# Retention's output stores issued from GpSimd instead of SyncE, and a rearranged turning of the first rows, in a streamed encoder block

## The chip, the cores and the metric

The kernel runs on one core of a Trainium2 chip. The metric is the device time of one execution in microseconds (us), taken as the median of several runs. TensorE is called PE here, VectorE DVE, ScalarE ACT, GpSimd POOL and SyncE SP, as the profile does.

## The reference

One layer of a hybrid encoder block over 2048 tokens of width 1024, all in float32. A norm, one wide projection, two branches (chunked attention and retention), two gated output projections, a merge, one more projection, the residual, and a norm at the end:

```python
h = rms_norm(x, norm_gain[l])
proj = jnp.einsum('bsd,df->bsf', h, w_in[l])
q_a, k_a, v_a, g_a, q_r, k_r, v_r, g_r, m_a, m_r = split_columns(proj)
o_a = chunk_band_attention(q_a, k_a, v_a, rel_bias[l])
branch_a = jnp.einsum('bsf,fd->bsd', o_a * jax.nn.silu(g_a), w_out_attn[l])
...
o_r = retention_chunkwise(qr, kr, v_r, gn_gain[l]) 
branch_r = jnp.einsum('bsf,fd->bsd', o_r * jax.nn.silu(g_r), w_out_ret[l])
mixed = jax.nn.sigmoid(m_a) * branch_a + jax.nn.sigmoid(m_r) * branch_r
x = x + jnp.einsum('bsd,de->bse', mixed, w_out[l])
return rms_norm(x, final_gain)
```

Retention is computed in chunks of 64 tokens with a state that is carried from chunk to chunk, and its output `o` is normalised by head: `(o - mean) * rsqrt(var + eps)`. The kernel sums the squares of `o` for that (`o2` below).

## The kernel before

All intermediate results that do not fit on the chip go through scratch tensors in device memory, and every stage streams its inputs back. Matrix products are done in pairs of a high and a low part of each float32 operand (`wh`, `wl`; `sh`, `sl`; `o2h`, `o2l`): ACT casts the high part, DVE or POOL subtracts it from the original for the low part, and PE multiplies high by high, low by high and high by low. The big projections (`ps_p_*`, `ps_g_*`, `ps_out_*`) use a seven-product scheme for two by two blocks.

**The order of work** is the order in which the program emits it: each engine runs its instructions strictly in that order. `fill(n)` emits n groups of projection matmuls, and between them stand the steps of attention or of retention, so that PE always has projection work while the other engines prepare the next step. `later(n, fn)` emits `fn` n groups later, and `put(n, dst, src)` (line 258) is `later` of a DMA on SP's queue.

**Buffers.** In each stage a ring of tiles of 128x512, made by `E(name)` (line 114), holds all short-lived values; in retention it has 12 of them (`E_RET`, line 57). A tile that is handed out again makes the first writer wait until everything that read or wrote the old content is through, a DMA that still reads it included. Which slot a new tile gets is decided when the program is built, and not by the source line alone.

**Start-up** (`start_up`, line 711). The first four row tiles `xa[0..3]` of x are loaded, each 128 tokens in two halves of 512 columns. `squares` takes the sum of squares (ACT one half, DVE or ACT the other), `chain` the reciprocal root (`n_a`), `scale` multiplies the rows by it, and `turn` transposes 128x128 blocks on PE into four tiles `pa0_0..3`. The norm weights `gains` (8x128) are transposed on PE too, and ACT writes them, times a constant, to `ng` (line 812). `hi` and `lo` then apply `ng` and split the turned rows into `R`, the operand of all projections; `prime(1)` (line 814) casts the first weights. PE has nothing to do until the rows come, so `spin(n)` gives it n transposes of the identity, whose result nobody reads. Before the change, the spare turns and the turned gains lie in one tile, called `gains`.

**Retention** (`retention`, line 632) runs twice, over the first and the second half of the tokens (at 560 to 720 us and 1306 to 1480 us), with 16 steps each: a step is one pair of heads and 256 tokens. In a step PE makes the scores `sr` of a coming step, DVE masks them (`sm`), ACT casts `sh`, POOL makes `sl`, and PE multiplies `sh` and `sl` with the values `vr` into `o`. `evacuate` (line 1777) then has ACT copy `o` to `oz` and its square to `o2` (shown as tile `o` too), stores `oz` to the scratch `ors` (256 KB, lines 1787 to 1791), and has ACT cast `o2h` and POOL make `o2l`, which PE sums into `ssq` in the next step. POOL also makes `t_g` and `wl_g` for the projection that fills the step. In the second half POOL issues eight DMAs of its own, `state<-sts` and `sstk<-sks`; all other loads and stores of retention are issued by SP.

Of the kernel before, what the change touches and what calls it, by code (L numbers as in the profile page):

```python
# [16 lines left out]
ALU = mybir.AluOpType  # L17
# [4 lines left out]
P = 128  # L22
SEQ = 2048
DM = 1024
# [49 lines left out]
def hybrid_kernel(  # L74
# [30 lines left out]
    def r32(ap):  # L105
        return ap.bitcast(F32)

    def ACC(name):
        return ps_acc.tile([P, 512], F32, tag="acc", name=name)
# [4 lines left out]
    def E(name, dt=F32, shape=(P, 512)):  # L114
        return epool[0].tile(list(shape), dt, tag="e", name=name)

    def TR(name):
        return xpool[0].tile([P, 512], F32, tag="tr", name=name)
# [34 lines left out]
    pe, act, dve, pool = Ordered(nc.tensor), Sometimes(nc.scalar), Sometimes(nc.vector), Sometimes(nc.gpsimd)  # L153
# [3 lines left out]
    ident = const.tile([P, P], F32, name="ident")  # L157
    make_identity(nc, ident)
    gn = const.tile([P, HEADS], F32, name="gn")
    ng = const.tile([P, 8], F32, name="ng")  # L160
# [84 lines left out]
    def later(n, fn):  # L245

        order[0] += 1
        deferred.append((steps[0] + n, order[0], fn, free[0]))
        deferred.sort(key=lambda e: e[:2])
# [8 lines left out]
    def put(lag, dst, src):  # L258

        later(lag, lambda: dma(dst, src))  # L260
# [355 lines left out]
    def prime(n):  # L616

        while ready[0] < min(n, len(seq)):
            _, ch, k = seq[ready[0]]
            ch.prepare(k)  # L620
            ready[0] += 1
            if ahead[0] and strict[0] and ready[0] + 1 < len(seq):
                _, ch, k = seq[ready[0] + 1]
                if isinstance(ch, Strassen):
                    ch.sums(k)
# [85 lines left out]
    def start_up():  # L711

        ch = jobs[0].chunks[:2]
        xa, xb = ([[E(f"x{i}_{t}_{f}") for f in range(2)] for t in range(4)] for i in "ab")
# [20 lines left out]
        nn = {i: [small.tile([P, 4], F32, tag=f"n{v}", bufs=2, name=f"n{v}_{i}") for v in range(4)] for i in "ab"}  # L735

        def squares(xs, i, t, on_dve=False, fs=range(2)):
            for f in fs:
                junk = junks[on_dve].bitcast(BF16)[:, 512 * f:512 * f + 512]
                if on_dve:  # L740
                    dve.tensor_tensor_reduce(
                        junk, xs[t][f], xs[t][f], 1.0, 0.0, ALU.mult, ALU.add, ss[i][:, t, f:f + 1]
                    )
                else:
                    act.activation(junk, xs[t][f], AF.Square, accum_out=ss[i][:, t, f:f + 1])

        def chain(i, t0, t1):
            deviation(ss[i][:, t0:t1], *(n[:, t0:t1] for n in nn[i]))

        def scale(xs, i, t, f, on_act=False):  # L750
            r = nn[i][0][:, t:t + 1]
            if on_act:
                act.mul(xs[t][f], xs[t][f], r)
            else:
                dve.tensor_scalar(xs[t][f], xs[t][f], r, None, ALU.mult)

        def turn(ps, k, xs, f, ts=range(4)):

            for t in ts:
                pe.transpose(ps[:, t * P:(t + 1) * P], xs[t][f][:, k * P:(k + 1) * P], ident)  # L760
# [13 lines left out]
        gains = E("gains")[0:8, 0:P]  # L774
# [11 lines left out]
            quarter(c, "b22")  # L786
            rows(xb, B, 2 + c)

        spare = ACC("gains")
        turned = spare[:, 0:8]  # L790

        def spin(n):
            for _ in range(n):
                pe.transpose(spare[:, P:2 * P], ident, ident)

        spin(38)
        ps = [TR(f"pa0_{k}") for k in range(4)]
        for t in (0, 1):
            squares(xa, "a", t, False, (0,))
            squares(xa, "a", t, True, (1,))  # L800
        chain("a", 0, 2)
        for t in (0, 1):
            scale(xa, "a", t, 0)
        for k in range(4):
            turn(ps[k], k, xa, 0, (0, 1))
        pe.transpose(turned, gains, ident[0:8, 0:8])
        spin(10)
        squares(xa, "a", 2)
        squares(xa, "a", 3, False, (0,))
        squares(xa, "a", 3, True, (1,))  # L810
        chain("a", 2, 4)
        act.mul(ng, turned, DM ** 0.5)
        scale(xa, "a", 2, 0)
        prime(1)
        scale(xa, "a", 3, 0, True)
        for k in range(4):
            turn(ps[k], k, xa, 0, (2, 3))
# [814 lines left out]
    def retention(s, ps_ret):  # L1632
# [8 lines left out]
        for n in range(3):  # L1641
            t = epool[0].tile([P, 2, 2, T], F32R, tag=f"q{n}", bufs=1, name=f"qr_{s}_{n}")
# [112 lines left out]
        def sure(here):  # L1755

            while not here():
                emit()
# [18 lines left out]
        def evacuate(p, st, ops):  # L1777
            b, un = st // 2, st % 2
            nm = f"{p}_{st}"
            got = []  # L1780

            def out_():
                oz = E(f"oz_{nm}")
                o2 = E(f"o2_{nm}")
                act.copy(oz, ops)
                act.activation(o2, ops, AF.Square)
                put(
                    2,
                    orscr[p][b][:, :, un * T:(un + 1) * T].rearrange("i p t -> p i t"),
                    oz.rearrange("p (i t) -> p i t", i=2),  # L1790
                )
                later(2, lambda: high(o2))

            def high(o2):
                got.append(E(f"o2h_{nm}", F32R))
                act.copy(got[0], o2)
                later(2, lambda: low(o2))

            def low(o2):
                got.append(E(f"o2l_{nm}", F32R))  # L1800
                pool.tensor_tensor(got[1], o2, r32(got[0]), ALU.subtract)

            later(1, out_)

            def sums():
                sure(lambda: len(got) == 2)
                r = 4 * p + st - 4 * s
                for n, t in enumerate(got):
                    pe.matmul(
                        ssq, ohr[:, ONE - r:ONE - r + 16], t, start=not begun[0],  # L1810
                        stop=(p == 3 and st == 4 * s + 3 and n == 1), skip_group_check=True,
                    )
                    begun[0] = True

            return sums
# [105 lines left out]
    for j in (jobs[0], jobs[2]):  # L1921
        for i in range(2):
            hook(j.name, i, 1 if j is jobs[2] else (0, 1, 1), lambda j=j, i=i: j.chunks[2].load([i]))
    start_up()
    ahead[0] = AHEAD

# [133 lines left out]
```

## Time and profile before

| what | value |
|---|---|
| median of 3 runs | 1889.68 us (1889.32 to 1890.17) |
| profiled execution | 1889.91 us, of which its span in the profile is 1888.1 us |
| PE busy | 1863.9 us (99% of the span) |
| DVE, ACT, POOL busy | 1367.6, 933.6 and 672.8 us |
| DMA queue of POOL (q0) | 448 packets, 1.05 MB |
| DMA queue of SP (q1) | 253552 packets, 363.28 MB |

All instructions come from helpers, so every row has the same line, L143, and is told apart by the names of its tiles (numbers are left out: `sl` stands for every tile whose name begins so). In a row of the timeline stand the start, the duration, the engine, the operation with output and inputs, and in brackets the idle time before it and what ended it. "DMA to landing" runs from the issue of a DMA to its last byte.

### The profile page before, as it was taken

The numbers are of one execution on the slowest core, as the hardware profiler recorded it, in microseconds if no ns is written. First come the engines' busy times: TensorE is split into PE (matmuls) and PEld (weight loads), VectorE is DVE, ScalarE is ACT, GpSimd is POOL, SyncE is SP. The second block draws the span as 40 slices with busy tenths as digits, with TensorE's granted clock in tenths as the row PEclk, the third lists the DMA queues.
The fourth block names the chain that finished last, engine by engine and source line by source line (L and its number), as shares of the span: only waits on it lengthen the run. The fifth ranks groups of instructions, "written<-read, shape, count | busy, mean of one in ns | idle before, by whom it ended". The sixth has DMA issues, their size and how long they took to land. (4 is left out here: it accounts for less than half of the span.)

```text
span 1888.1 us, 30822 instructions
## 1 busy us (share of the span) xinstructions
PE 1863.9 (99%) x10197; PEld 1603.3 (85%) x10197; DVE 1367.6 (72%) x2464; ACT 933.6 (49%) x1931; POOL 672.8 (36%) x604
## 2 busy tenths in 40 slices
PE   9999999999999999999999999999999999999998
PEld 7899889888888888799889888888888888888886
DVE  6879888677656658889798677765656766767665
ACT  7555554666654555443333666664455321223544
POOL 0102106455646562001105545555564100002775
PEclk9999999999999999999999999999999999999999
DMA  6586886666559987776776656555999999986674
GB/s 201 163 287 188 278 274 216 186 190 190 178 150 271 272 236 261 235 224 200 223 251 198 193 151 187 178 152 143 273 267 292 312 357 345 324 299 219 210 224 142
DMA packets 319295, 431.58 MB, mean 229 GB/s; under 512 B 28360, under 2 KB 193056, under 8 KB 319136
## 3 DMA queue, kind: packets, MB, share of 16 engines
q1 hardware_dynamic: 253552, 363.28, 60.0%
q10 hardware_dynamic: 65136, 65.28, 11.5%
q8 instruction: 81, 1.33, 0.3%
q0 software_dynamic: 448, 1.05, 0.2%
q14 instruction: 78, 0.64, 0.1%
HBM read 283.93 MB, written 145.57 MB: 227 GB/s over the span
## 5 line engine op out<-in xcount | busy, mean ns | idle before, releaser
L143 POOL TENSOR_SCALAR pr<-pr,rsum 128x640 f32<-128x640 f32 (+4 forms) x128 | 99.5, 777 | 195.5 <-DVE rsum L143 141.9
L143 DVE TENSOR_TENSOR ptl<-tp,pth 128x512 fp32r<-128x512 f32 (+1 forms) x168 | 100.2, 597 | 92.1 <-ACT pth L143 75.3
L143 ACT ACTIVATE pr<-pr,mn 128x640 f32<-128x640 f32 (+4 forms) x128 | 98.0, 765 | 122.2 <-DVE mn L143 96.2
L143 PE MATMUL ps_g_x<-r,wh_g 128*128 128x512 f32 x448 | 141.3, 397 | 1.2 <-ACT u_g L143 1.1
L143 PE MATMUL ps_g_z<-r,wh_g 128*128 128x512 f32 x448 | 141.4, 397 | 0.3 <-DVE c_g L143 0.3
L143 POOL TENSOR_TENSOR l_vr<-vrt,h_vr 128x512 fp32r<-128x512 f32 x32 | 47.8, 1495 | 200.6 <-ACT h_vr L143 147.0
L143 POOL TENSOR_TENSOR t_out<-raw_out 128x512 f32<-128x512 f32 x7 | 14.1, 2011 | 260.4 <-DVE wl_out L143 260.4
L143 DVE CUSTOM_DVE_ANT_0 pr<-wide,bt 128x640 f32<-128x640 f32 (+4 forms) x128 | 93.6, 732 | 16.6 <-PE wide L143 14.1
L143 ACT CAST pth<-tp 128x512 fp32r<-128x512 f32 (+1 forms) x168 | 85.2, 507 | 37.5 <-PE tp L143 32.3
L143 PE MATMUL wide<-ka,qa 128*128 128x384 f32 (+1 forms) x448 | 95.1, 329 | 2.0 <-DVE mn L143 2.0
L143 ACT CAST wh_p<-raw_p 128x512 fp32r<-128x512 f32 x111 | 68.0, 618 | 50.5 <-PE ps_p_y L143 16.7
L143 PEld LDWEIGHTS tp<-ident,pr 128*128 128x128 f32 x560 | 71.6, 140 | 24.7 <-POOL pr L143 2.3
L143 PEld LDWEIGHTS ps_g_x<-r,wh_g 128*128 128x128 f32 x448 | 79.8, 188 | 14.7 <-ACT u_g L143 2.5
L143 PEld LDWEIGHTS ps_g_z<-r,wh_g 128*128 128x128 f32 x448 | 79.8, 189 | 13.6 <-DVE c_g L143 0.7
L143 PE MATMUL tp<-ident,pr 128*128 128x128 f32 x560 | 89.2, 272 | 1.4 <-POOL pr L143 1.2
L143 DVE TENSOR_TENSOR sm<-sr,dm 128x384 f32<-128x384 f32 x64 | 35.5, 555 | 75.7 <-PE sr L143 33.5
L143 PE MATMUL ps_g_z<-r,wl_g 128*128 128x512 f32 x224 | 88.2, 394 | 0.0
L143 PE MATMUL ps_g_x<-r,wl_g 128*128 128x512 f32 x224 | 88.2, 394 | 0.0
L143 DVE TENSOR_TENSOR wl_p<-raw_p,wh_p 128x512 fp32r<-128x512 f32 x111 | 79.5, 722 | 10.8 <-ACT wh_p L143 10.3
L143 POOL TENSOR_TENSOR wl_g<-t_g,wh_g 128x512 fp32r<-128x512 f32 x56 | 75.5, 1349 | 27.9 <-ACT wh_g L143 26.4
L143 POOL TENSOR_TENSOR t_g<-raw_g,t_g 128x512 f32<-128x512 f32 x56 | 73.9, 1321 | 23.9 <-POOL t_g L143 4.6
L143 POOL TENSOR_TENSOR sl<-sm,sh 128x384 fp32r<-128x384 f32 x64 | 69.9, 1092 | 33.6 <-ACT sh L143 12.4
(935 smaller groups left out, 6026.0 us busy)
## 6 DMA issues: line engine op xcount, KB each, us to landing
raw_g<-in_w_in_dram ACTq DMA_DIRECT2D x56, 512.0 KB, 4.8
raw_p<-in_w_in_dram ACTq DMA_DIRECT2D x50, 512.0 KB, 6.0
qa<-qas SPq DMA_DIRECT2D x128, 128.0 KB, 3.2
vr<-vrs SPq DMA_DIRECT2D x32, 512.0 KB, 5.8
ka<-kas SPq DMA_DIRECT2D x56, 256.0 KB, 4.3
va<-vas SPq DMA_DIRECT2D x40, 256.0 KB, 3.1
kds<-kdt_k SPq DMA_DIRECT2D x32, 256.0 KB, 4.3
vas<-vat SPq DMA_DIRECT2D x64, 128.0 KB, 4.2
```

The lines of the kernel that those rows point to most:

```text
L143: return tc.keep_in_program_order(op(*a, **k))
```

## The change

In start-up, the spare turns get a tile of their own, `spare`, apart from `turned`; there are 37 and 8 of them instead of 38 and 10; the transpose of the gains moves ahead of the turning of the first rows; the second row tile is scaled on POOL instead of DVE; and ACT's `ng` comes behind `prime(1)`. In retention, the store of `oz` is issued by POOL.

```diff
-        spare = ACC("gains")
-        turned = spare[:, 0:8]
+        turned = ACC("gains")[:, 0:8]
+        spare = ACC("spare")
 
         def spin(n):
             for _ in range(n):
-                pe.transpose(spare[:, P:2 * P], ident, ident)
-
-        spin(38)
+                pe.transpose(spare[:, 0:P], ident, ident)
+
+        spin(37)
+        pe.transpose(turned, gains, ident[0:8, 0:8])
...
         chain("a", 0, 2)
-        for t in (0, 1):
-            scale(xa, "a", t, 0)
+        scale(xa, "a", 0, 0)
+        pool.tensor_scalar(xa[1][0], xa[1][0], nn["a"][0][:, 1:2], 1.0, ALU.mult, ALU.mult)
         for k in range(4):
             turn(ps[k], k, xa, 0, (0, 1))
-        pe.transpose(turned, gains, ident[0:8, 0:8])
-        spin(10)
+        spin(8)
...
-        act.mul(ng, turned, DM ** 0.5)
         scale(xa, "a", 2, 0)
         prime(1)
+        act.mul(ng, turned, DM ** 0.5)
         scale(xa, "a", 3, 0, True)
...
                 act.copy(oz, ops)
                 act.activation(o2, ops, AF.Square)
-                put(
-                    2,
+                later(2, lambda: pool.dma_start(
                     orscr[p][b][:, :, un * T:(un + 1) * T].rearrange("i p t -> p i t"),
                     oz.rearrange("p (i t) -> p i t", i=2),
-                )
+                ))
                 later(2, lambda: high(o2))
```

The order of instructions on ACT in start-up, before. `r50` is the first cast weight (`prime(1)`), `xa_3_0` the fourth row tile, `ng` the norm weights, and `r00` the high part of the turned rows:

```order
L143 ACTIVATE n2_a_467<-n3_a_468 128x2 [waits DVE_49]
L143 ACTIVATE ng_78<-gains_503 128x8 [waits PE_49]
L143 CAST r50_90<-raw_f0_460 128x512 [waits DMAHW0_49]
L143 ACTIVATE xa_3_0_448<-xa_3_0_448,n0_a_465 128x512 [waits DVE_49,Activation_49]
L143 ACTIVATE r00_80<-pa0_0_542,ng_78 128x512 [waits PE_49]
```

And in the changed program:

```order
L143 ACTIVATE n2_a_467<-n3_a_468 128x2 [waits DVE_49]
L143 CAST r50_90<-raw_f0_460 128x512 [waits DMAHW0_49]
L143 ACTIVATE ng_78<-gains_503 128x8 [waits PE_49]
L143 ACTIVATE xa_3_0_448<-xa_3_0_448,n0_a_465 128x512 [waits DVE_49,Activation_49]
L143 ACTIVATE r00_80<-pa0_0_543,ng_78 128x512 [waits PE_49]
```

`ng` and the cast have changed places, and what `ng` waits for on PE is now the transpose ahead of the row turns, no longer the last spare turn in the same tile.

The second place is POOL in the first steps of retention's first half (`ors` is the scratch, `oz` what is stored, the first two numbers in `o2l_0_0` and `sl_0_1_1` the pair of heads and the step). Before:

```order
L143 TENSOR_TENSOR sl_0_1_0_7355<-sm_0_1_0_7319,sh_0_1_0_7331 128x384 [waits Activation_49,Pool_49]
L143 TENSOR_TENSOR t3_g0_9_7400<-raw_g0_9_0_7111,raw_g0_9_1_7176 128x512
L143 TENSOR_TENSOR o2l_0_0_7427<-o2_0_0_7358,o2h_0_0_7384 128x512 [waits PE_49,Activation_49,Pool_49]
L143 TENSOR_TENSOR sl_0_1_1_7429<-sm_0_1_1_7361,sh_0_1_1_7386 128x384 [waits PE_49,Activation_49]
L143 TENSOR_TENSOR sl_0_2_0_7478<-sm_0_2_0_7431,sh_0_2_0_7442 128x384 [waits PE_49,Activation_49]
L143 TENSOR_TENSOR o2l_0_1_7536<-o2_0_1_7470,o2h_0_1_7495 128x512 [waits PE_49,Activation_49,Pool_49]
L143 TENSOR_TENSOR sl_0_2_1_7538<-sm_0_2_1_7473,sh_0_2_1_7497 128x384 [waits DMAHW6_49,PE_49,Activation_49]
```

And in the changed program:

```order
L143 TENSOR_TENSOR sl_0_1_0_7353<-sm_0_1_0_7317,sh_0_1_0_7329 128x384 [waits Activation_49,Pool_49]
L143 DMA ors_0_0_293<-oz_0_0_7355 128x2x256 [waits Activation_49]
L143 TENSOR_TENSOR t3_g0_9_7398<-raw_g0_9_0_7109,raw_g0_9_1_7174 128x512
L143 TENSOR_TENSOR o2l_0_0_7425<-o2_0_0_7356,o2h_0_0_7382 128x512 [waits DMASW2_49,PE_49,Activation_49]
L143 TENSOR_TENSOR sl_0_1_1_7427<-sm_0_1_1_7359,sh_0_1_1_7384 128x384 [waits Activation_49,Pool_49]
L143 TENSOR_TENSOR sl_0_2_0_7476<-sm_0_2_0_7429,sh_0_2_0_7440 128x384 [waits PE_49,Activation_49]
L143 DMA ors_0_0_293<-oz_0_1_7467 128x2x256 [waits Activation_49]
L143 TENSOR_TENSOR o2l_0_1_7534<-o2_0_1_7468,o2h_0_1_7493 128x512 [waits DMASW3_49,Activation_49]
L143 TENSOR_TENSOR sl_0_2_1_7536<-sm_0_2_1_7471,sh_0_2_1_7495 128x384 [waits PE_49,Activation_49]
```

Beside the two stores, the waits have changed: the tile of `o2l` has been given the slot of the `oz` that has just been stored, and `o2l` now waits for `DMASW2` and `DMASW3`, the semaphores of POOL's own DMAs, which are raised when the store has landed.

Of the 32 stores, POOL itself is the first to wait for the landing of 24, mostly in the step of the store: thirteen times in `o2l` and eleven times in `sl`. Of the other eight, three are first waited for on DVE about half a step later, and the rest after retention or several steps on.

## The prediction

> **What bounds the kernel now.** The page first, for what the change can win at all:
>
> ```profile
> span 1888.1 us, 30822 instructions
> PE 1863.9 (99%) x10197; PEld 1603.3 (85%) x10197; DVE 1367.6 (72%) x2464; ACT 933.6 (49%) x1931; POOL 672.8 (36%) x604
> ```
>
> PE is busy all but 24.2 us of the span. The change takes no matrix product away (it drops three of 48 spare turns and adds none), so it can only win where PE waits, and lose wherever it makes PE wait anew. About 0.2% (3.8 us) is what a measurement of this kernel can tell from no change. So I read, next, what PE waits for in the two places that the change touches: the first 30 us, and the first of retention's two stretches.
>
> ```profile
> PE pa L143 <- ACT xa L143: 1.0, 1, 1.0
> PE pa L143 <- DVE xa L143: 0.6, 1, 0.6
> ...
> PE o L143 <- ACT o L143: 1.6, 1, 1.6
> PE o L143 <- POOL sl L143: 1.0, 2, 0.8
> PE ssq L143 <- POOL o2l L143: 0.3, 1, 0.3
> ```
>
> The columns are who waits for whom, us in total, times, longest. The first two are from the start, the others from retention. No wait on a load stands in either list. That is the whole prize: 1.0 us in front, and 2.9 us in the 160 us of retention. Now what fills retention:
>
> ```profile
> 560.00:600.00 40.00, 40.00 (x227) 34.46 (x226) 23.41 (x44) 20.84 (x40) 22.23 (x19) 1.00 0.96 287
> 680.00:720.00 40.00, 38.06 (x212) 31.72 (x212) 23.49 (x44) 20.09 (x39) 21.79 (x18) 1.00 0.68 207
> ```
>
> Columns: window, its length, busy us of PE, PEld, DVE, ACT and POOL, clock, DMA share, GB/s. POOL is half idle there, so it has room for issues; the DMA engines are nearly full, at 0.96, so a transfer there doesn't land quickly whoever issues it.
>
> **The front.** Where PE waits for the fourth row tile:
>
> ```profile
> 8.27 0.88 DVE L143 TENSOR_SCALAR xa<-xa,n_a 128x512 f32<-128x512 f32 x2
> 9.07 0.69 DVE L143 CUSTOM_DVE_ANT_0 junk<-xa 128x512 bf16<-128x512 f32 x1
> 10.28 1.31 PE L143 MATMUL gains<-ident 128*128 128x128 f32 x10
> 10.89 0.16 DVE L143 SCALAR_TENSOR_TENSOR n_a<-n_a 128x2 f32<-128x2 f32 x1
> 11.63 0.18 ACT L143 ACTIVATE ng<-gains 128x8 f32<-128x8 f32 x1 [1.36 <-PE gains L143]
> 11.70 0.61 ACT L143 CAST r<-raw_f 128x512 fp32r<-128x512 f32 x1
> 12.21 0.72 ACT L143 ACTIVATE xa<-xa,n_a 128x512 f32<-128x512 f32 x1
> 12.98 0.98 PE L143 MATMUL pa<-ident,xa 128*128 128x128 f32 x7 [1.03 <-ACT xa L143]
> ```
>
> ACT stands idle for 1.36 us because `ng` waits until the spare turns, in the same tile, are through at 11.59; the cast and the scaling of the tile queue behind it. With tiles of their own, and the gains turned first, cast and `ng` fit into that idle time, and the scaling can begin when `n_a` is there, at 10.89 + 0.16 = 11.05 instead of 12.21: 1.16 us earlier. Of the two scalings (0.88) one leaves DVE, so the square sum at 9.07, and `n_a` behind it, could come 0.4 earlier still: a gain of at most 1.55. Two spare turns less ahead of the third tile (2 x 0.13) keep PE from being the next that is late: eight end near 11.3.
>
> Against this stands the scaling on POOL, which no row of before shows. Nearest are POOL's scalings in attention and, for two engines side by side, a DVE row beside POOL's `o2l` and the same operation six microseconds before, alone:
>
> ```profile
> L143 POOL TENSOR_SCALAR pr<-pr,rsum 128x640 f32<-128x640 f32 (+4 forms) x128 | 99.5, 777 | 195.5 <-DVE rsum L143 141.9
> ...
> 584.54 0.68 DVE L143 TENSOR_TENSOR wl_g<-t_g,wh_g 128x512 fp32r<-128x512 f32 x1
> 590.81 1.65 DVE L143 TENSOR_TENSOR wl_g<-raw_g,wh_g 128x512 fp32r<-128x512 f32 x1
> ```
>
> DVE took 1.65 instead of 0.68: it was held for about as long as POOL's operation ran. If the square sum is held likewise until POOL's 0.7 us, begun at 8.7 behind DVE's scaling, are over at 9.4, it starts 0.33 later than before, and the gain shrinks to 1.16 - 0.33 = 0.8. I take 0.8, since this holding is a thing the trace shows; bounds 0.3 (PE held on the second tile as well) and 1.55.
>
> **SP and POOL as issuers.** The issue of a store leaves SP and comes to POOL:
>
> ```profile
> L143 SPq DMA_DIRECT2D ors<-oz x16: 370/378/384, 578.2 to 715.2; - x16
> ...
> L143 POOL DMA_DIRECT2D sstk<-sks x4: 560/568/572, 1307.3 to 1424.0; - x4
> ```
>
> SP's later loads are issued 0.4 us earlier per step, and no longer wait behind `oz`; PE waits for none of them, so that is worth nothing. POOL gets 32 x 0.57 = 18 us more; a step's store is followed by 3.64 us of idle time in the row of 590.61 below, which covers it. If that cover is gone, the 0.57 falls on `sl`, and is counted in the waits that follow.
>
> **The new wait.** This is the dear part. In the changed order `o2l` or `sl` takes the slot of the `oz` just stored, in the same step, and so waits until the store has landed. One step, the second:
>
> ```profile
> 585.95 0.59 ACT L143 COPY oz<-o 128x512 f32<-128x512 f32 x1
> 585.95 1.02 POOL L143 TENSOR_TENSOR sl<-sm,sh 128x384 fp32r<-128x384 f32 x1 [1.64 <-PE o L143]
> 590.61 1.30 POOL L143 TENSOR_TENSOR o2l<-o,o2h 128x512 fp32r<-128x512 f32 x1 [3.64 <-PE o L143]
> 591.86 1.48 POOL L143 TENSOR_TENSOR sl<-sm,sh 128x384 fp32r<-128x384 f32 x1
> 594.47 0.28 PE L143 MATMUL o<-sl,vr 128*128 128x256 f32 x1
> ```
>
> POOL can issue the store at 586.97, when `sl` is done. `o2l` then starts at 590.61 as before, if the store has landed. Behind it on POOL is the `sl` that PE takes at 594.47; it ends at 593.34, so there are 1.13 us to spare. The store may take 590.61 + 1.13 - 586.97 = 4.77 us; each microsecond beyond holds PE by one, and the next `oz`, and so the next store, as much. The tightest is the fourteenth:
>
> ```profile
> 698.88 0.59 ACT L143 COPY oz<-o 128x512 f32<-128x512 f32 x1 [3.83 <-POOL sl L143]
> 702.27 1.55 POOL L143 TENSOR_TENSOR o2l<-o,o2h 128x512 fp32r<-128x512 f32 x1
> 703.78 1.01 POOL L143 TENSOR_TENSOR sl<-sm,sh 128x384 fp32r<-128x384 f32 x1
> 705.07 0.28 PE L143 MATMUL o<-sl,vr 128*128 128x256 f32 x1
> ```
>
> There the room is 0.28 us, so 702.27 + 0.28 - 699.52 = 3.03. Worked out in the same way, of the 24 steps in which POOL waits for its own store, one waits too late to matter, and the others allow 3.0, 3.5, 4.3, six times 4.7 to 4.9, five times 5.1 to 5.9, and nine times 6.2 to 7.5 us. The sum of what is over is 0.2 us for a landing time of 3.2, 1.4 for 4.0, 3.8 for 4.8, 10.2 for 5.4, and 18.6 for 6.0. The curve is steep, and the landing time decides.
>
> What the trace has on that:
>
> ```profile
> ors<-oz SPq DMA_DIRECT2D x32, 256.0 KB, 5.4
> sstk<-sks POOLq DMA_DIRECT2D x4, 128.0 KB, 5.7
> oas<-oa POOLq DMA_DIRECT2D x2, 128.0 KB, 2.3
> state<-sts POOLq DMA_DIRECT2D x4, 64.0 KB, 4.8
> ```
>
> Size and median us to landing are the last columns. `oas` is issued by POOL at the end of attention, before retention's loads, and is the lower bound: 2.3 for 128 KB, and for twice the bytes some 0.9 more, 3.2. `sstk` has `state` ahead of it on its own queue; with SP's store, which has SP's loads ahead of it, it makes the upper end, 5.4 to 5.7. `state` is nearest in what matters: issued by POOL within retention, nothing of its own queue ahead, 4.8. Twice its bytes behind it (`sstk`) cost only 0.9, so its size is less of a worry than the load it meets. I take 4.8.
>
> [...]
>
> **What goes.** Before, some waiters stood behind SP's stores already, and two gave stalls:
>
> ```profile
> 697.84 1.00 POOL L143 TENSOR_TENSOR sl<-sm,sh 128x384 fp32r<-128x384 f32 x1 [1.54 <-DMA ors<-oz]
> 700.01 0.51 PE L143 MATMUL o<-qr,sstk 128*128 128x256 f32 x2 [1.62 <-ACT o L143]
> 658.10 0.39 PE L143 MATMUL o<-sl,vr 128*128 128x256 f32 x1 [0.81 <-POOL sl L143]
> ```
>
> The first: SP's store of step 13 landed at 697.7, `sl` and behind it `oz` were late, PE stood for 1.62. The second came in the same way from the store of step 9. Slots and queue are others now, and both should go: 1.62 + 0.81 = 2.4 us.
>
> **The sum**, against the profiled execution of 1889.91 us (1888.1 of span, 1.8 around it): - 0.8 in front, - 2.4 of old stalls, + 3.8 of new ones: + 0.6, 1890.5. That execution lies 0.2 above the median of 1889.68, so 1890.3 is the forecast.
>
> **Rivals.**
> 1. The stores land at 4.0 to 5.1 us, the forecast: what is won is given back. Between - 1.8 and + 3.7. For it: `state`. Chance 0.42.
> 2. Stores land as in an idle queue, at 3.2: - 0.8 - 2.4 + 0.2 = - 3.0, 1886.7; with the front's best value - 3.75, 1885.9. For it: `oas`; a queue of its own is not behind SP's loads. Against: `state` was not quick on that same queue. Chance 0.18, of which 0.08 for more than 0.2% faster.
> 3. Stores land as SP's did, 5.4: + 10.2 - 3.2 = + 7.0, 1896.7; at 6.0 it is + 15.4, 1905.1. POOL becomes the engine that PE waits for in each second step. It decides from 5.14 us on, where the new stalls reach 7.0. For it: `ors` and `sstk`, both at 256 KB or behind 64, and the DMA share of 0.96; a spread of landing times also costs more than their mean, since the curve bends up. Against: rooms of 6 us and over in nine steps, and less load per us once steps grow longer. Chance 0.36.
> 4. The front gives nothing, since POOL's scaling holds DVE and PE, or the first weights come late anyway, with retention as in the forecast: + 1.4, 1891.1. Chance 0.04.
>
> **The numbers.** Faster by over 0.2%: 0.08, from rival 2. Within: 0.42 + 0.10 + 0.04 = 0.56. Slower: 0.36. The range runs from a landing time of 3.2 with the usual front (1886.7) to about 5.75 (new stalls of 15, 1901.5), as cases of up to 2 in 10 beyond are left out. The likeliest case alone has 1887.9 to 1893.4.
>
> **What would show it.** Right: in the profile after, PE's wait for `xa` in front at 0.3 or below, and the turn that begins at 12.98 near 12.2; POOL's `o2l` and `sl` ended by DMA `ors` in half of the steps of retention; PE's waits for `o2l`, `sl` or `o` at 3 to 5 us over both stretches, at other places than 658 and 700; the stores' median landing near 4.8. Wrong: a median under 4 or over 5.4, waits that stand there without PE standing behind them, or old stalls still at 658 and 700.

## The result and the profile after

The changed kernel takes 1922.41 us (median of 5 runs, 1921.2 to 1931.07), before 1889.68: a ratio of 1.0178, with a 95% interval of 1.0165 to 1.0191. The forecast was 1890.3 and its range ended at 1901.5, so it was wrong by 32 us.

The page of the changed kernel, its first lines and the row of POOL's DMA queue:

```profile
span 1920.6 us, 30863 instructions
PE 1878.1 (98%) x10194; PEld 1609.1 (84%) x10194; DVE 1360.7 (71%) x2463; ACT 933.3 (49%) x1931; POOL 696.4 (36%) x637
...
q0 software_dynamic: 3008, 9.44, 1.4%
```

The span grew by 32.5 us. PE is idle for 42.5 us instead of 24.2, which is 18.3 more. But PE is also *busy* for 14.2 us longer, with the same matrix products. The loss has two parts. Where they lie is shown by the windows of the two stretches of retention, cut so that they hold nearly the same work. First before, then after:

```profile
560.00:725.00 165.00, 161.03 (x909) 136.11 (x909) 97.57 (x182) 83.33 (x162) 95.89 (x80) 1.00 0.85 252
1306.00:1490.00 184.00, 183.42 (x1011) 155.55 (x1010) 112.06 (x195) 93.05 (x178) 97.51 (x88) 1.00 0.91 278
```

```profile
560.00:745.00 185.00, 170.42 (x910) 141.19 (x910) 97.03 (x182) 82.54 (x161) 106.17 (x95) 0.96 0.76 224
1325.00:1525.00 200.00, 191.20 (x1020) 160.01 (x1019) 110.84 (x198) 91.93 (x177) 106.86 (x100) 0.98 0.83 258
```

In the first stretch the same 910 matrix instructions (909 before) need 20 us more: PE is idle 14.6 instead of 4.0 us, and busy 170.4 instead of 161.0. The column behind POOL is the granted clock: 0.96 and 0.98, where it was 1.00. What PE waited for in the first stretch, and what POOL waited for there:

```profile
PE ssq L143 <- POOL o2l L143: 7.8, 5, 3.3
PE o L143 <- POOL sl L143: 3.8, 9, 1.4
PE o L143 <- ACT o L143: 2.2, 1, 2.2
```

```profile
POOL o2l L143 <- DMA ors<-oz: 22.8, 5, 7.1
```

That is the wait which the prediction described, at its place. One step of it in the timeline, the second, which the prediction took as its example:

```profile
587.46 0.58 ACT L143 COPY oz<-o 128x512 f32<-128x512 f32 x1
588.33 0.74 POOL L143 DMA_DIRECT2D ors<-oz  x1 [0.49 <-ACT oz L143]
596.19 1.25 POOL L143 TENSOR_TENSOR o2l<-o,o2h 128x512 fp32r<-128x512 f32 x1 [7.12 <-DMA ors<-oz]
597.41 1.00 POOL L143 TENSOR_TENSOR sl<-sm,sh 128x384 fp32r<-128x384 f32 x1
597.50 0.40 PE L143 MATMUL ssq<-o2l,ohr 128*16 128x512 f32 x1 [3.34 <-POOL o2l L143]
```

The store was issued at 588.33, landed 7.7 us later, and `o2l` had to wait for it for 7.12 us; PE stood for 3.34 us at `ssq`. And what came behind this wait, in windows of the same columns as above:

```profile
590.00:598.00 8.00, 4.66 (x28) 3.64 (x26) 2.61 (x6) 1.45 (x3) 1.81 (x2) 1.00 0.78 242
598.00:605.20 7.20, 6.99 (x25) 5.96 (x24) 1.49 (x5) 3.72 (x8) 5.84 (x6) 0.53 0.79 261
605.20:615.00 9.80, 9.60 (x56) 7.97 (x55) 4.77 (x9) 4.76 (x10) 6.58 (x6) 1.00 0.56 154
```

For 7.2 us after the wait PE runs at a granted clock of 0.53, and does 25 instructions, where the following 9.8 us hold 56. This PE wait cost twice: its own 3.34 us, and about half of the 6.8 us of half clock behind it. By its clock records, the trace of the changed kernel has five such stretches in retention, at a granted clock of 0.50, 3.4 or 6.8 us each and 20.5 us together, so 10.2 us, half of them, are lost to the clock by my estimate. Before has none there.

The start of the changed kernel, and the first product of before for comparison:

```profile
7.88 0.48 DVE L143 TENSOR_SCALAR xa<-xa,n_a 128x512 f32<-128x512 f32 x1
8.02 0.90 POOL L143 TENSOR_SCALAR xa<-xa,n_a 128x512 f32<-128x512 f32 x1 [5.68 <-ACT junk L143]
8.77 0.69 DVE L143 CUSTOM_DVE_ANT_0 junk<-xa 128x512 bf16<-128x512 f32 x1 [0.41 <-DMA xa<-in_x_dram]
8.97 0.98 PE L143 MATMUL pa<-ident,xa 128*128 128x128 f32 x7 [0.23 <-POOL xa L143]
10.38 0.17 ACT L143 ACTIVATE ng<-gains 128x8 f32<-128x8 f32 x1
12.73 0.49 PE L143 MATMUL ps_p_(0, 0)_614<-r,r 128*128 128x512 f32 x1
```

```profile
14.09 0.50 PE L143 MATMUL ps_p_(0, 0)_616<-r,r 128*128 128x512 f32 x1
```

From the first scaling to the first product it is 12.73 - 7.88 = 4.85 us, before 14.09 - 8.27 = 5.82: the front is 1.0 us shorter.

### The profile page after: what moved, and what is told of

It reads as the page before. It is cut to its first block, busy times and chain, and to the rows that moved or that the text cites. A ratio compares the mean times of both kernels' runs of the same rounds, so it can differ in the third digit from the quotient of the medians.

```text
span 1920.6 us, 30863 instructions
## 1 busy us (share of the span) xinstructions
PE 1878.1 (98%) x10194; PEld 1609.1 (84%) x10194; DVE 1360.7 (71%) x2463; ACT 933.3 (49%) x1931; POOL 696.4 (36%) x637
## 5 line engine op out<-in xcount | busy, mean ns | idle before, releaser
L143 DVE CUSTOM_DVE_ANT_0 pr<-wide,bt 128x640 f32<-128x640 f32 (+4 forms) x128 | 93.6, 731 | 16.8 <-PE wide L143 13.7
```

The source lines that it names most:

```text
L143: return tc.keep_in_program_order(op(*a, **k))
```

## The experiments

Theory A: the whole loss is the wait for the landing, which comes from the shared slot of the ring, with what a long PE wait does to the clock. Theory B, the rival: issuing on POOL is itself what costs (32 issues of 0.73 us in the way of `o2l` and `sl`, and a slower kind of DMA).

**The two parts apart.** Run e1_front has the edit of start-up alone and the store on SP; e2_store has the edit of `evacuate` alone.

```diff
 # e1_front: the change without
-                later(2, lambda: pool.dma_start(
+                put(2, ...)
 # e2_store: before with
-                put(2, ...)
+                later(2, lambda: pool.dma_start(
```

> The change's first part alone (start-up), the store back on SP. In the changed kernel's trace the first product starts at 12.73 us, 1.36 earlier than before, of which 0.4 is that the rows themselves came earlier in that execution. If the parts are separate: 1.0 us faster, about 1888.7. Rival, the front has cost something too (POOL's scaling took 0.90 us): 1890 or more.

> The change's second part alone (the store on GpSimd), the start-up as before. If the whole loss is in retention and the parts add: about 1923.4, with PE idle 18 us longer than before and some 20 us of half clock. If the front is a part of the loss: clearly below 1920.

Measured: 1888.64 us (before, on the same chip, 1890.43; ratio 0.9989, 0.9980 to 0.9998) and 1927.21 us (ratio 1.0197, 1.0178 to 1.0216). The front is a small gain, and the whole loss comes with the store. It is some 4 us more than I had expected of the store alone, and why was not followed up. A second run of the front alone, e10_front_again, gave 1887.9 against 1889.69 (0.9987, 0.9978 to 0.9996).

> The start-up alone once more, beside the two others on one chip: 1.0 to 1.8 us under before.

**The wait taken away, the issue on POOL kept** (e3_own_slot). `oz` gets a slot that only the next `oz` takes, nine microseconds later. The ring gives up one tile for it.

```diff
-E_RET = 12
+E_RET = 11
-                oz = E(f"oz_{nm}")
+                oz = epool[0].tile([P, 512], F32, tag="oz", bufs=1, name=f"oz_{nm}")
 # and the store on POOL, as in the change
```

> The store on GpSimd as in the change, start-up as before, but oz has a slot of its own (one, and the ring 11 instead of 12), so no POOL instruction waits for the landing of the store; only the next step's oz does, 9 us later. Theory A (the wait for the landing, by the shared slot, is the loss): back to 1888 to 1892. Theory B (issuing on POOL is the loss: 32 issues of 0.73 us ahead of o2l and sl, 23 us of POOL's time): 1905 or more.

Measured: 1889.27 us against 1890.43 (0.9994, 0.9985 to 1.0002). The 38 us of e2_store are gone, with the same 32 issues on POOL and the same kind of DMA. The stores' time to landing and PE's waits in the first stretch:

```profile
DMA to landing us min/median/max: 2.5/5.3/8.3
```

```profile
PE ssq L143 <- POOL o2l L143: 1.5, 2, 1.1
PE ps_g_x L143 <- ACT u_g L143: 0.7, 1, 0.7
PE o L143 <- POOL sl L143: 0.4, 2, 0.2
```

The row of landings also counts SP's loads of `ors` later on; the stores alone have a median of 5.7 us. They land no sooner than in the change, but no POOL or DVE work waits for them, so PE doesn't either.

**The wait put in, the issue on SP kept** (e4_sp_forced). `oz` and the `o2l` of its step share one slot.

```diff
+                oz = epool[0].tile([P, 512], F32, tag="zo", bufs=1, name=f"oz_{nm}")
...
+                got.append(epool[0].tile([P, 512], F32, tag="zo", bufs=1, name=f"o2l_{nm}").bitcast(F32R))
 # the ring 11 instead of 12, the store put on SP as before
```

> The store on SP as before, start-up as before, but o2l is put into the slot of the oz of its own step (one slot for the two, the ring 11), so that o2l waits for the store to land in all 32 steps. Theory A: the loss is there without any issue on POOL; with SP's median landing of 5.4 us in all steps 1915 to 1935, with half-clock stretches behind the longest PE waits. Theory B: within 3 us of before, 1887 to 1893.

Measured: 1936.2 us (1.0240, 1.0226 to 1.0254). The loss is there, 1 us above the range that I had expected and larger than the change's, without one store on POOL. Who waited for the store, and PE's wait in the first stretch:

```profile
POOL o2l L143: 130.6, 25
```

```profile
PE ssq L143 <- POOL o2l L143: 13.2, 8, 4.0
```

Both ways Theory B is ruled out as the cause: the wait brings the loss with either issuer, and without it neither has one (that the ring of 11 costs nothing by itself is shown by e9_sp_own_slot below).

**The price of the issue by itself** (e7_pool_issues_beside). The store stays on SP, and POOL issues another DMA beside it, which nobody waits for.

```diff
+                later(2, lambda: pool.dma_start(
+                    spscr[4 * p + st % 4].rearrange("p (n c) -> p n c", n=4),
+                    ident.unsqueeze(1).to_broadcast([P, 4, P]),
+                ))
                 put(2, ...)
```

> Before, with the store on SP, and beside it in each of the 32 steps one more DMA issued by GpSimd: the identity (64 KB, in 512 descriptors' worth of 512 B) is written four times into a scratch that nobody reads (256 KB more traffic per step); it prices the issue on POOL and the traffic without any wait for a landing. Theory A: within 3 us of before, since the 20 to 25 us of POOL's time lie in its idle time. Theory B: 10 us or more slower.

Measured: 1893.47 us against 1889.66 (1.0017, 1.0008 to 1.0026), so 3.8 us, a little over the 3 us of Theory A and far from the 10 of Theory B. The DMAs' issue took 0.726 us, as in the change, and in the profiled execution PE's wait at the old place near 700 us was 2.1 us instead of 1.6, with one stretch of half clock (3.4 us) behind it. Whether the rest is the issue or the 8 MB of added traffic was not separated; e3_own_slot, with as many issues and no added traffic, has no such cost.

**Does a PE wait bring the half clock?** (e8_gaps) Before, with POOL kept busy ahead of `o2l` in four steps, and no DMA added.

```diff
+                for _ in range({(0, 2): 6, (1, 1): 9, (2, 0): 12, (2, 3): 15}.get((p, st), 0)):
+                    pool.tensor_tensor(held, ident, ident, ALU.add)
                 pool.tensor_tensor(got[1], o2, r32(got[0]), ALU.subtract)
```

> Before, with POOL held up by 6, 9, 12 and 15 additions of the 128x128 identity (their sum is read by nobody) ahead of o2l in four far apart steps of the first stretch, no DMA involved. It tests whether a PE wait itself brings the half clock. If it does: PE waits of about 1, 2, 3 and 4 us, the longer ones followed by 3.4 or 6.8 us of half clock, and a time that grows by the waits and half of the half-clock stretches, 10 + 5 = 15 us. If the half clock comes from something else in the change: the waits alone, 10 us, at full clock.

Measured: 1904.81 us, 15.2 over before (1.0076, 1.0063 to 1.0090). The four PE waits were 3.07, 1.05, 1.45 and 3.11 us, not graded as I had expected, since the steps' rooms differ. With the two of 3.1 us came 6.8 us of half clock each, beginning 0.5 and 1.0 us before the wait's end, and none came with the two short ones: 8.7 + 13.7 / 2 = 15.5 us of new loss. The profiled execution was a shorter one (1902.37 us, its span 12.5 us longer than before's): PE is idle 6.5 us more there, since the two old stalls of before are not in it, and busy 6.0 us more. The first of the two:

```profile
602.88 0.40 PE L143 MATMUL ssq<-o2h,ohr 128*16 128x512 f32 x1
606.34 0.61 PE L143 MATMUL ssq<-o2l,ohr 128*16 128x512 f32 x1 [3.07 <-POOL o2l L143]
609.29 1.16 PE L143 MATMUL ps_g_v<-r,wh_g 128*128 128x512 f32 x2
```

```profile
605.80:612.60 6.80, 6.26 (x23) 5.58 (x24) 0.56 (x1) 3.63 (x7) 3.65 (x4) 0.51 0.46 138
```

**A version faster than both**, though under before by less than 0.2%. e5_both_own_slot is the whole change with `oz` in a slot of its own; e6_front_sp_own_slot the same with the store on SP; e9_sp_own_slot is before with the own slot alone.

```diff
 # e5: the change, e6: e1_front, e9: before, each with
-E_RET = 12
+E_RET = 11
-                oz = E(f"oz_{nm}")
+                oz = epool[0].tile([P, 512], F32, tag="oz", bufs=1, name=f"oz_{nm}")
```

> The whole change (start-up too, store on GpSimd), with oz in a slot of its own. If front and own slot add, as their single runs have them (1.8 and 1.2 us under before in the same series): 3.0 us under before. If the front's gain or the old stalls are shared or noise: 1 to 2 us under before.

> The changed start-up, store on SP as before, oz in a slot of its own. If it was the slot that removed the old stalls, and the issuing engine is worth nothing: the same time as with the store on GpSimd, within 1 us, about 3 us under before. If the issuing on GpSimd has a worth of its own: 1 us or more slower than that, near 1.8 us under before.

> Before with one edit: oz in a slot of its own (ring 11), store on SP, start-up as before. If the old stalls at 658 and 700 us are the waits for the stores' landing: they go, 1 to 2 us under before, the same as with the store on GpSimd and a slot of its own. If the issuing on GpSimd was what helped there: no difference from before.

> The whole change with oz in a slot of its own once more, beside the start-up alone: if the two gains add, 1 us or more under the start-up alone; if what the slot removes is seldom late anyway, within 0.5 us of it.

| run | us | before, same series | ratio, 95% interval |
|---|---|---|---|
| e5_both_own_slot | 1888.16 | 1889.66 | 0.9989, 0.9980 to 0.9998 |
| e6_front_sp_own_slot | 1888.09 | 1889.66 | 0.9990, 0.9981 to 0.9999 |
| e9_sp_own_slot | 1888.67 | 1889.69 | 0.9988, 0.9979 to 0.9997 |
| e11_both_again (the kernel of e5) | 1887.35 | 1889.69 | 0.9983, 0.9974 to 0.9992 |

With a slot of its own for `oz`, it makes no difference who issues the store: e5 and e6 are 0.07 us apart. The own slot alone takes 1.0 us off before (0.6 to 4.0 by its interval). The best version is 1.5 to 2.3 us under before, but only 0.6 us under the front alone in the same series (1887.9), inside the intervals. That the two gains add is therefore not shown.

## Why the prediction was wrong

- **What bounds the kernel, and that PE's idle time is the only prize: right, but half of the account.** I reckoned losses as PE's idle time alone. That PE may run slower when it isn't idle, as at the clock of 0.53 behind the wait of 3.34 us, was no term of the sum.
- **The front, - 0.8: right.** The trace has 1.0, and e1_front and e10_front_again 1.8 each, with intervals of 0.4 to 3.8 and 0.8 to 4.2 us. The reason for choosing 0.8 held only in part, so that the number came this close is partly luck. In the change's trace the square sum on DVE waited for its data until 8.77, when POOL's scaling had 0.15 us to go, and took its usual 0.69. Where it began earlier beside the scaling, it took longer: in e6_front_sp_own_slot 0.32 us before POOL's end,

```profile
8.82 0.86 DVE L143 CUSTOM_DVE_ANT_0 junk<-xa 128x512 bf16<-128x512 f32 x1 [0.24 <-DMA xa<-in_x_dram]
```

  and in e10_front_again 0.42 us before it, for 0.96 us. That is 0.2 to 0.3 us, where 0.33 was reckoned. Of the fourth rival, PE held on the second tile, 0.23 us came true.
- **SP as issuer, nothing: right** (e5 against e6). **POOL's issue: 0.57 predicted, 0.73 measured** (the store has 256 rows of 1 KB, `sstk` 128; what sets the time was not tested); of no weight, as e3_own_slot shows.
- **Old stalls, - 2.4: half right, and of no use in the change.** The one at 700 us has no counterpart there (nor in e1_front and e10_front_again, with the store on SP). The one at 658 us, from the landing of the ninth store, came back larger, as the row of 676.07 below shows. Both go when `oz` has its own slot (e9_sp_own_slot: 1.0 us gained, with one new wait of 1.1 us for an `o2l`).
- **The new wait: the mechanism right, and this is the term that was mis-sized, + 3.8 instead of some 36.** (By the same sum: 32.5 us of longer span, and the 1.0 and 2.4 of the other two terms.) The landing time was nearly right, 4.8 taken and 5.1 measured:

```profile
ors<-oz POOLq DMA_DIRECT2D x32, 256.0 KB, 5.1
```

  At that median my curve gives about 6 to 7. Four things were missing from it. First the spread: the landings run from 2.5 to 7.8 us, and the mean of the curve over the 32 of them is some 12 us, an estimate from the rooms as the prediction groups them. I had named this in the third rival, and priced it at nothing. Secondly, I counted only stores which POOL waits for. The ninth store, first waited for by DVE, cost PE 2.2 us:

```profile
672.29 0.56 DVE L143 TENSOR_TENSOR sm<-sr,dm 128x384 f32<-128x384 f32 x1 [5.57 <-DMA ors<-oz]
...
676.07 0.51 PE L143 MATMUL o<-qr,sstk 128*128 128x256 f32 x2 [2.23 <-ACT o L143]
```

  These two make some 14 us. The PE idle time measured is 18.8 us more than before in the two stretches (10.6 and 8.2), and some 21 with the old stalls that went. What the other 7 us are stays open. Thirdly, I took each step's room from before, as if every step began undisturbed, which may be a part of them, but no run tests it. Stores that go out late are no sign of it: in the steps 7, 11, 19 and 23 the store was issued 3.1 to 3.8 us after `oz` in the change, and 2.2 to 3.6 us after it in e3_own_slot, where no POOL work waits for a store. Fourthly, the half clock: 10.2 us, with no counterpart in the prediction; e8_gaps, with no DMA added, has it with the waits of 3.07 and 3.11 us, 6.8 us each. Over the whole span that is 18.3 us of PE idle time and 10.2 of the 14.2 us of longer busy time. The other 4.0 are busy time at full clock; matrix products that begin behind a wait are longer in the rows (0.39 instead of 0.28 us for `o<-sl`), which fits, but was not measured apart.
- **The rivals.** By its condition the first came, at its very edge: the stores' median is 5.05 us in the trace, and the case ended at 5.1. The course was the third's, with POOL as the engine that PE waits for, at nearly five times its price of 7, although its condition ("from 5.14 us on") was just not reached. So it was not the landing time that failed but the price put on it. The second (3.2 us) didn't come: a queue of its own gave the store no quicker landing, 5.1 on POOL and 5.4 on SP.
- **What would show it.** `o2l` and `sl` were ended by DMA `ors` in 13 of the 32 steps, where half had been written. In front the turns of the fourth tile came earlier, as written, but PE's wait for `xa` ahead of them was 0.50 us and not 0.3 or below. "3 to 5 us over both stretches" failed (those waits are some 22 us), and with it the forecast.

## What to carry to other kernels

When a store moves to another engine's queue, look at which instruction the allocator hands the stored tile to: here the slot of the stored tile went to one of the next instructions on the same engine, and one slot of its own took a loss of 38 us away. In this kernel, whose TensorE is 99% busy, a wait that holds it sometimes cost more than its own length; single waits in retention of 1.67 us and more also came with 3.4 or 6.8 us at half clock in every case here. And where a cost bends upwards with a time that scatters, reckon with the scatter, not with the median: here some 12 us instead of 6 or 7, which was still the smaller part of the miss.

## What the runs showed of the hardware

The half clock (a granted clock of 0.50 in the records) came with every single PE wait in retention of 1.67 us and more (the shortest in e1_front, 1.67; in the change 2.07, 2.23, 2.48 and 3.34; in e8_gaps 3.07 and 3.11; the longest in e4_sp_forced, 3.97). It came with none of the other single waits, the longest of them 1.62 us in before. With pairs of shorter waits close together it came in some places (0.91 and 0.65 in the change, 1.24 and 0.45 and 1.59 and 0.38 in e4_sp_forced) and not in others (the same 0.91 and 0.65 in e2_store, 0.96 and 0.65 in e4_sp_forced). Each stretch was 3.41 or 6.83 us long.

The clock records and PE's rows together show what it goes with. In every trace the times from one change of the clock to the next are whole multiples of 3.413 us (in the change 174, 2, 8, 1, 12, 1, 201 of them and so on, the stretches of half clock 3413 or 6827 ns), as if on a fixed grid. Let PE's idle time be summed within the cells of this grid, over retention in all thirteen traces: each of the 19 cells at full clock with 1.67 to 3.10 us of idle time was followed by half clock (in the change 2.66, 1.94, 2.23 and 2.07 us). Of the cells with less, one was (1.57 us, the pair in the change), and the others were not, the fullest of them at 1.66 us. So in these traces the half clock went with a cell that was idle for about half of its length or more, and not with a wait's own length. In e2_store the border of two cells lies between the 0.91 and the 0.65 us, and in before it cuts the stall of 1.62 us into 0.92 and 0.70. Outside retention there is, but for the end of every trace, when PE has finished, one more such stretch, at the start of e9_sp_own_slot, behind a cell with 1.43 us. Why a stretch is one cell or two long is not shown.

The cells in retention that half clock followed were half to nine tenths idle (1.57 to 3.10 of 3.413 us), none of them wholly, and all but two of the single waits that it came with (3.51 in e2_store and 3.97 in e4_sp_forced) were shorter than a cell.

POOL's scaling of a 128x512 tile took 0.90 us at the start, and DVE's square sum beside it took 0.69 us with 0.15 us of overlap, 0.86 with 0.32 (e6_front_sp_own_slot) and 0.96 with 0.42 (e10_front_again). In retention, in before, DVE's `wl_g` took 1.65 us beside POOL's `o2l` and 0.68 alone.
